# A row sum streamed through one core: one row per partition loaded ahead of the blocks, fifteen left for the end

## The chip, the core and the metric

The kernel runs on one core of one Trainium2 chip. The metric is the device time of one execution in microseconds (us); lower is better. Three engines matter: VectorE (DVE in the profile), ScalarE (ACT) and SyncE (SP), which issues all transfers on one queue. The transfers themselves are carried out by the core's 16 DMA engines.

## The reference

```python
batch, seq, dim = 32, 512, 1024
x = np.random.randn(batch, seq, dim).astype(np.float32)
multiplier = 0.5

def reference(x, multiplier):
    return (np.sum(x, axis=-1) * multiplier).astype(np.float32)
```

So 16,384 rows of 1,024 floats (4 KB a row, 64 MB in all) are each summed and scaled, and 64 KB of results go back.

## The kernel before

**Tiling.** With 128 partitions, each partition has 128 rows (`rows`), cut into eight blocks of `B = 16` rows. The first `own = 112` rows of each partition are consecutive rows of x, so that partition p begins at row 112 p (`x_rows`); seven blocks come from there. A block is one load of 128 pieces of 64 KB (8 MB), and consecutive partitions read 448 KB apart. The remaining 2,048 rows of x are the eighth block (`x_last`): 16 consecutive rows per partition, 64 KB apart. Results go back the same way: `out_rows` for the first 112 columns of `res`, `out_last` for the last 16.

**Buffers.** Three buffers `xb0` to `xb2` of 64 KB per partition take turns. Block b's load waits until VectorE has reduced block b - 3. `sums` holds raw sums, `res` the scaled results, 128 columns each. A small tile `end` holds the last columns of the last row.

**Loads.** The helper `load` (L73 to L82) makes one transfer on SyncE's queue, with up to two waits: `free` (VectorE has read the buffer's former contents) and `behind` (an earlier load has landed). All loads show line L76. When the program is finished, `start_loads_at_entry` moves SyncE's leading loads, those that wait for nothing, into the program's entry block, ahead of the barrier that the engines pass there. In the kernel before, these are the loads of blocks 0, 1 and 2.

**The seven blocks.** For blocks 0 to 5, VectorE reduces the whole block in one instruction (L121) and scales the 16 sums into `res` (L127). Of block 6 VectorE takes eight rows in this way, and ScalarE the other eight with `act_row` (L85): one activation per row that multiplies by the constant and accumulates.

**The tail.** The eighth block comes in five loads, in this order: ten rows, four rows, then one row and 384 columns of the last row, then 352 and 288 columns of it into `end`. Their edges are `bounds` and `cuts`. Before them stands a wait of SyncE for block 4's reduction, whose buffer they use. The third also waits for block 5's reduction, the second for block 5's landing, the fourth for block 6's landing and the fifth for block 6's reduction. Then SyncE issues the early store, 112 columns of `res` (L169), which waits for the last scaled sums of VectorE and the last of ScalarE's eight rows. In the tail `on_act` lists the rows that go to ScalarE; the others go to VectorE with `dve_sum` (L95), which adds a row's halves and accumulates. The last row is summed in three parts; the third (`final`) folds the earlier two in. The last store, 16 columns of `res` (L195), waits for `final` and for ScalarE's last row, and SyncE ends by waiting for both stores.

Of the kernel before, what the change touches and what calls it, by code (L numbers as in the profile page):

```python
# [9 lines left out]
def kernel(  # L10
# [13 lines left out]
    nc = tc.nc  # L24
# [4 lines left out]
    P = nc.NUM_PARTITIONS  # L29
# [3 lines left out]
    x_flat = x.flatten_outer_dims()  # L33
    N, D = x_flat.shape
    rows = N // P
    out_flat = out.rearrange("b s -> (b s)")
    mul = float(multiplier)

    B = 16
    n_blocks = rows // B  # L40
    assert N == P * rows and rows == n_blocks * B
    own = rows - B
    x_rows = x_flat[0 : P * own, :].rearrange("(p c) d -> p c d", p=P)
    x_last = x_flat[P * own : N, :].rearrange("(p c) d -> p c d", p=P)
    out_rows = out_flat[0 : P * own].rearrange("(p c) -> p c", p=P)
    out_last = out_flat[P * own : N].rearrange("(p c) -> p c", p=P)

    def sbuf(name, *shape):
        return ctx.enter_context(nc.sbuf_tensor(name, list(shape), fp32)).ap()
# [2 lines left out]
    buf = [sbuf(f"xb{i}", P, B, D) for i in range(bufs)]  # L52
    sums = sbuf("sums", P, rows)
    res = sbuf("res", P, rows)
    cuts = [384, 736, D]
    at = 368
    end = sbuf("end", P, at + D - cuts[1])

    def sem(name):
        return nc.alloc_semaphore(name=name)  # L60
# [5 lines left out]
    def marks(i, engine):  # L66

        s = dve_done if engine == "dve" else act_done
        i.then_inc(s, 1)
        counts[engine] += 1  # L70
        return counts[engine]

    def load(name, dst, src, free=None, behind=None):  # L73

        landed = sem(name)
        i = nc.sync.dma_start(out=dst, in_=src)  # L76
        if free is not None:
            i.wait_op(dve_done, free, "sem-ge")
        if behind is not None:
            i.wait_op(behind, 16, "sem-ge")  # L80
        i.then_inc(landed, 16)
        return landed  # L82

    def act_row(t, r, col):
        return nc.scalar.activation(  # L85
            out=t[:, r, :],
            in_=t[:, r, :],
            func=mybir.ActivationFunctionType.Copy,
            scale=mul,
            accum_out=res[:, col : col + 1],  # L90
        )

    def dve_sum(row, dst, scale):
        mid = row.shape[-1] // 2
        return nc.vector.tensor_tensor_reduce(  # L95
            out=row[:, 0:mid],
            in0=row[:, 0:mid],
            in1=row[:, mid:],
            scale=scale,
            scalar=0.0,  # L100
            op0=ADD,
            op1=ADD,
            accum_out=dst,
        )

    freed = []
    blocks = []
    for b in range(n_blocks - 1):
        c0 = b * B
        t = buf[b % bufs]  # L110
# [11 lines left out]
                out=sums[:, c0 : c0 + h], in_=t[:, 0:h, :], axis=mybir.AxisListType.X  # L122
# [5 lines left out]
            out=res[:, c0 : c0 + h],  # L128
            in_=sums[:, c0 : c0 + h],
# [12 lines left out]
    t = buf[(n_blocks - 1) % bufs]  # L142
    nc.sync.wait_ge(dve_done, freed[n_blocks - 1 - bufs])
    flat = t.rearrange("p c d -> p (c d)")
    flat_last = x_last.rearrange("p c d -> p (c d)")
    bounds = [0, 10 * D, 14 * D, 15 * D + cuts[0]]

    landed = [
        load(f"landed_p{k}", flat[:, lo:hi], flat_last[:, lo:hi], free, behind)
# [7 lines left out]
        )  # L157
    ]
    landed_end = [
        load(f"landed_e{k}", end[:, to : to + hi - lo], x_last[:, B - 1, lo:hi], free, behind)  # L160
        for k, (to, lo, hi, free, behind) in enumerate(
            (
                (0, cuts[0], cuts[1], None, blocks[n_blocks - 2]),
# [7 lines left out]
    early_stored = sem("early_stored")  # L171
    early.then_inc(early_stored, 16)

    on_act = {1, 4, 7, 9, 13, 14}
    for k, (lo, hi) in enumerate(((0, 10), (10, 14), (14, 15))):
        on = [r for r in range(lo, hi) if r in on_act]
        nc.scalar.wait_ge(landed[k], 16)
        for r in on:
            i = act_row(t, r, c0 + r)
        late_act = marks(i, "act") if k == len(landed) - 1 else None  # L180
        on = [r for r in range(lo, hi) if r not in on_act]
        nc.vector.wait_ge(landed[k], 16)
        for r in on:
            dve_sum(t[:, r, :], res[:, c0 + r : c0 + r + 1], mul)
    dve_sum(t[:, B - 1, 0 : cuts[0]], end[:, at - 2 : at - 1], 1.0)
    nc.vector.wait_ge(landed_end[0], 16)
    second = dve_sum(end[:, 0 : cuts[1] - cuts[0]], end[:, at - 1 : at], 1.0)

    second.then_inc(landed_end[1], 1)
    final = dve_sum(end[:, at - 2 :], res[:, rows - 1 : rows], mul)  # L190
    final.wait_op(landed_end[1], 17, "sem-ge")
    done = marks(final, "dve")

    nc.sync.wait_ge(act_done, late_act)
    store = nc.sync.dma_start(out=out_last, in_=res[:, own:])  # L195
    store.wait_op(dve_done, done, "sem-ge")
    stored = sem("stored")
    store.then_inc(stored, 16)
    nc.sync.wait_ge(early_stored, 16)
    nc.sync.wait_ge(stored, 16)  # L200

    def start_loads_at_entry(nc_):
# [61 lines left out]
```

## Time and profile before

| What | us |
|---|---|
| Runs: median of 3 (lowest to highest) | 160.75 (160.7 to 160.75) |
| The profiled execution: span from its first to its last instruction | 159.3 |
| VectorE busy | 119.8 (75%) |
| ScalarE busy | 16.3 (10%) |
| DMA queue of SyncE: share of the 16 engines' span | 98.1% |
| HBM read 67.11 MB, written 0.07 MB: mean rate over the span | 422 GB/s |

The page's parts used here are the chain of work that ended last, followed back from the last instruction; the timeline, which lists instructions in order of time with the idle time before each and what ended it; the issues of transfers with their size and the time from issue to landing; and the trace's records of DMA packets (start, duration, bytes). One packet here is the piece that goes to one partition. The slices of the DMA's busy share on the page swing between 6 and 9 tenths because a packet of 64 KB is counted where it starts; they are not stalls.

### The profile page before, as it was taken

What the parts mean: (1) busy time and instruction counts of PE and PEld (TensorE: products, weight loads), DVE (VectorE), ACT (ScalarE), POOL (GpSimd) and SP (SyncE); (2) the same over time, 40 slices, a digit from 0 to 9 for tenths busy, and PEclk for the clock granted to TensorE, in tenths of its full rate; (3) what the DMA queues carried; (4) which work ended last, traced back from release to release, by engine and by line L of the source; (5) the groups of instructions that cost most, each with busy time, mean ns of one, the idle gap of its engine ahead of it and who ended that gap; (6) DMA issues with size and microseconds to landing.
All of it is one profiled execution on the core that took longest, in us unless ns stands there. A gap on an engine that the chain in (4) does not pass through costs nothing.

```text
span 159.3 us, 123 instructions
## 1 busy us (share of the span) xinstructions
DVE 119.8 (75%) x38; ACT 16.3 (10%) x29; POOL 0.2 (0%) x4
## 2 busy tenths in 40 slices
DVE  0000059998699968999599995999959999598376
ACT  3000000000000000000000000000000000397384
POOL 0000000000000000000000000000000000000000
DMA  7996996997998969969969969969989799798994
GB/s 263 526 526 263 526 526 263 526 477 313 526 428 362 526 280 510 526 263 526 526 263 526 526 263 526 494 296 526 444 345 526 345 444 526 329 473 350 424 396 151
DMA packets 2016, 67.18 MB, mean 422 GB/s; under 512 B 480, under 2 KB 736, under 8 KB 864
## 3 DMA queue, kind: packets, MB, share of 16 engines
q1 hardware_dynamic: 2016, 67.18, 98.1%
HBM read 67.11 MB, written 0.07 MB: 422 GB/s over the span
## 4 chain that ended last, share of the span: by engine, by line
DMA 74%; DVE 24%; another core or an unknown queue 1%; SPq 0%; issue 0%
DMA xb<-in_x_dram 74%; DVE sums L121 22%; DVE xb L95 1%; DVE end L95 0%; SPq L76 0%; DVE res L127 0%; DVE res L95 0%
## 5 line engine op out<-in xcount | busy, mean ns | idle before, releaser
L121 DVE TENSOR_REDUCE sums<-xb 128x16 f32<-128x16384 f32 (+1 forms) x7 | 112.0, 16001 | 33.3 <-DMA xb<-in_x_dram 33.3
L85 ACT ACTIVATE xb<-xb 128x1024 f32<-128x1024 f32 x14 | 14.6, 1044 | 139.1 <-DMA xb<-in_x_dram 139.1
L95 DVE CUSTOM_DVE_ANT_0 xb<-xb 128x512 f32<-128x512 f32 (+1 forms) x10 | 6.0, 655 | 4.4 <-DMA xb<-in_x_dram 4.4
L85 ACT ACTIVATION_READ_ACCUMULATOR xb<-xb 128x1 f32 x14 | 2.6, 187 | 0.0
L85 ACT ACT_TABLE_LOAD x1 | 1.3, 1283 | 2.4 <-PEq L26 2.4
L127 DVE TENSOR_SCALAR res<-sums 128x16 f32<-128x16 f32 (+1 forms) x7 | 1.2, 174 | 0.2
L95 DVE DVE_READ_ACCUMULATOR2_ANT res<- 128x1 f32 x10 | 0.8, 82 | 0.0
L95 DVE CUSTOM_DVE_ANT_0 end<-end 128x176 f32<-128x176 f32 (+1 forms) x2 | 0.7, 326 | 0.0
L95 DVE DVE_READ_ACCUMULATOR2_ANT end<- 128x1 f32 x2 | 0.2, 82 | 0.0
L245 POOL MEMSET const-bfloat16-1.0<- 128x1 bf16 x1 | 0.1, 101 | 0.0
L245 POOL MEMSET const-uint8-127<- 128x1 uint8 x1 | 0.1, 101 | 0.0
L245 POOL MEMSET const-float32-0.0<- 128x1 f32 x1 | 0.1, 98 | 0.2 <-issue 0.2
L245 POOL MEMSET const-float32-1.0<- 128x1 f32 x1 | 0.1, 98 | 0.0
## 6 DMA issues: line engine op xcount, KB each, us to landing
xb<-in_x_dram SPq DMA_DIRECT2D x1, 5120.0 KB, 33.6
xb<-in_x_dram SPq DMA_DIRECT2D x1, 2048.0 KB, 36.4
xb<-in_x_dram SPq DMA_DIRECT2D x1, 704.0 KB, 20.8
end<-in_x_dram SPq DMA_DIRECT2D x1, 176.0 KB, 19.2
end<-in_x_dram SPq DMA_DIRECT2D x1, 144.0 KB, 10.8
xb<-in_x_dram SPq DMA_DIRECT2D x7, 40.8
out_dram<-res SPq DMA_DIRECT2D x1, 56.0 KB, 10.6
out_dram<-res SPq DMA_DIRECT2D x1, 8.0 KB, 1.4
```

The source lines that it names most:

```text
L85: return nc.scalar.activation(out=t[:, r, :], in_=t[:, r, :], func=mybir.ActivationFunctionType.Copy, scale=mul, accum_out=res[:, col : co ...
L95: return nc.vector.tensor_tensor_reduce(out=row[:, 0:mid], in0=row[:, 0:mid], in1=row[:, mid:], scale=scale, scalar=0.0, op0=ADD, op1=ADD, ...
L121: nc.vector.reduce_sum(out=sums[:, c0 : c0 + h], in_=t[:, 0:h, :], axis=mybir.AxisListType.X),
L127: scaled = nc.vector.tensor_single_scalar(out=res[:, c0 : c0 + h], in_=sums[:, c0 : c0 + h], scalar=mul, op=mybir.AluOpType.mult,)
L245: nc = _bacc.Bacc("TRN2", target_bir_lowering=False, num_devices=1)
```

## The change

One row per partition is taken out of the tail and put in front. The first 128 rows of x, consecutive, go one to each partition into a new tile `head` (512 KB in 128 pieces of 4 KB). This load stands first on SyncE's queue and waits for nothing, so it is moved to the entry block together with those of blocks 0, 1 and 2. ScalarE sums it before all else, into the last column of `res`. The seven blocks follow as before, starting 128 rows later. The tail has 15 rows per partition, 60 KB apart: nine rows, four, one and 384 columns, 352 columns, 288 columns. ScalarE gets one row less in the tail's first piece; VectorE gets as many as before. A second early store sends the 128 results of `head`, 4 bytes from each partition, to the first 512 bytes of the output. The last store has 15 columns instead of 16, and SyncE waits for three stores at the end.

```diff
     own = rows - B
-    x_rows = x_flat[0 : P * own, :].rearrange("(p c) d -> p c d", p=P)
-    x_last = x_flat[P * own : N, :].rearrange("(p c) d -> p c d", p=P)
-    out_rows = out_flat[0 : P * own].rearrange("(p c) -> p c", p=P)
-    out_last = out_flat[P * own : N].rearrange("(p c) -> p c", p=P)
+    tail = B - 1
+    x_head = x_flat[0:P, :]
+    x_rows = x_flat[P : P + P * own, :].rearrange("(p c) d -> p c d", p=P)
+    x_last = x_flat[P + P * own : N, :].rearrange("(p c) d -> p c d", p=P)
+    out_head = out_flat[0:P].rearrange("(p c) -> p c", p=P)
+    out_rows = out_flat[P : P + P * own].rearrange("(p c) -> p c", p=P)
+    out_last = out_flat[P + P * own : N].rearrange("(p c) -> p c", p=P)
...
+    head = sbuf("head", P, 1, D)
...
+    landed_head = load("landed_head", head[:, 0, :], x_head)
+    nc.scalar.wait_ge(landed_head, 16)
+    marks(act_row(head, 0, rows - 1), "act")
+
...
-    bounds = [0, 10 * D, 14 * D, 15 * D + cuts[0]]
+    bounds = [0, 9 * D, 13 * D, 14 * D + cuts[0]]
...
-        load(f"landed_e{k}", end[:, to : to + hi - lo], x_last[:, B - 1, lo:hi], free, behind)
+        load(f"landed_e{k}", end[:, to : to + hi - lo], x_last[:, tail - 1, lo:hi], free, behind)
...
+    early_head = nc.sync.dma_start(out=out_head, in_=res[:, rows - 1 :])
+    head_stored = sem("head_stored")
+    early_head.then_inc(head_stored, 16)
+
-    on_act = {1, 4, 7, 9, 13, 14}
-    for k, (lo, hi) in enumerate(((0, 10), (10, 14), (14, 15))):
+    on_act = {1, 4, 7, 12, 13}
+    for k, (lo, hi) in enumerate(((0, 9), (9, 13), (13, 14))):
...
-    dve_sum(t[:, B - 1, 0 : cuts[0]], end[:, at - 2 : at - 1], 1.0)
+    dve_sum(t[:, tail - 1, 0 : cuts[0]], end[:, at - 2 : at - 1], 1.0)
...
-    final = dve_sum(end[:, at - 2 :], res[:, rows - 1 : rows], mul)
+    final = dve_sum(end[:, at - 2 :], res[:, rows - 2 : rows - 1], mul)
...
-    store = nc.sync.dma_start(out=out_last, in_=res[:, own:])
+    store = nc.sync.dma_start(out=out_last, in_=res[:, own : rows - 1])
...
     nc.sync.wait_ge(early_stored, 16)
+    nc.sync.wait_ge(head_stored, 16)
     nc.sync.wait_ge(stored, 16)
```

## The prediction

> **What bounds the kernel now.** I read the chain of waits first, then the timeline, the SyncE queue's own timeline, the DMA issues, and last the trace's packet records. From the page (the chain, its first two lines):
>
> ```profile
> DMA 74%; DVE 24%; another core or an unknown queue 1%; SPq 0%; issue 0%
> DMA xb<-in_x_dram 74%; DVE sums L121 22%; DVE xb L95 1%; DVE end L95 0%; SPq L76 0%; DVE res L127 0%; DVE res L95 0%
> ```
>
> Taken at its word, this gives VectorE (DVE) a quarter of the span. The timeline (start, duration, engine, line, operation, and in brackets the idle time before it and who ended it) corrects that:
>
> ```profile
> 21.81 17.22 DVE L121 TENSOR_REDUCE sums<-xb 128x16 f32<-128x16384 f32 x1 [21.81 <-DMA xb<-in_x_dram]
> ...
> 41.15 17.22 DVE L121 TENSOR_REDUCE sums<-xb 128x16 f32<-128x16384 f32 x1 [1.91 <-DMA xb<-in_x_dram]
> ...
> 118.56 17.22 DVE L121 TENSOR_REDUCE sums<-xb 128x16 f32<-128x16384 f32 x1 [1.92 <-DMA xb<-in_x_dram]
> ...
> 137.91 8.69 DVE L121 TENSOR_REDUCE sums<-xb 128x8 f32<-128x8192 f32 x1 [1.92 <-DMA xb<-in_x_dram]
> ...
> 150.03 0.69 DVE L95 CUSTOM_DVE_ANT_0 xb<-xb 128x512 f32<-128x512 f32 x1 [3.23 <-DMA xb<-in_x_dram]
> ...
> 154.93 0.69 DVE L95 CUSTOM_DVE_ANT_0 xb<-xb 128x512 f32<-128x512 f32 x1 [1.13 <-DMA xb<-in_x_dram]
> ...
> 156.67 1.06 ACT L85 ACTIVATE xb<-xb 128x1024 f32<-128x1024 f32 x1 [0.59 <-DMA xb<-in_x_dram]
> ...
> 157.50 0.31 DVE L95 CUSTOM_DVE_ANT_0 end<-end 128x145 f32<-128x145 f32 x1
> ...
> 157.89 0.34 SPq L195 DMA_DIRECT2D out_dram<-res  x1
> ```
>
> Every block starts on VectorE after about 1.9 us of idleness that a landing ends. Landings are 19.35 us apart (137.91 - 21.81 = 116.10 over six blocks): 1.209 us for each row per partition (4 KB per partition, 512 KB over all). So one uninterrupted stream of loads sets the time, with four terms: the first landing, 2.46 us later than one block of stream (21.81 - 19.35); the stream; 0.41 us from the last landing (about 157.48) to the store's issue at 157.89; and 1.46 us to the end of the span at 159.35.
>
> The SyncE queue, at its start and towards the end:
>
> ```profile
> 0.00 1.34 SPq L76 DMA_DIRECT2D xb<-in_x_dram  x3
> ```
>
> ```profile
> 137.90 9.05 SPq L76 DMA_DIRECT2D end<-in_x_dram  x2
> 147.06 0.37 SPq L169 DMA_DIRECT2D out_dram<-res  x1
> 157.89 0.34 SPq L195 DMA_DIRECT2D out_dram<-res  x1
> ```
>
> The issues run far ahead of the data, except the last store. The DMA issues (KB each, us from issue to landing) show that a queued transfer's wait is not its cost:
>
> ```profile
> out_dram<-res SPq DMA_DIRECT2D x1, 56.0 KB, 10.6
> out_dram<-res SPq DMA_DIRECT2D x1, 8.0 KB, 1.4
> ```
>
> The 56 KB store took 10.6 us because five loads stood before it; the 8 KB one met an empty queue.
>
> **The change, part by part.** The bytes read are the same, so only where they lie and how they are cut can matter.
>
> *One row moves from the tail's first piece to a load of its own.* Removed: one of ten rows, 1.209 us. Added: a one-row load in 4 KB packets. Its extra comes from the tail. Ten rows took 12.12 us (150.03 - 137.91) against 12.09 by rate, 0.03 over; four rows 4.90 against 4.84, 0.06 over; 1.375 rows 1.74 against 1.66, 0.08 over. The packet records say why: each of the 16 engines takes 8 packets per load, and mean packet times are 2418 ns for 64 KB (steady), 613 for 16 KB, 218 for 5632 B, 60 for 1408 B, 51 for 1152 B. That is about 27.2 bytes per ns plus 8 to 10 ns a packet. Eight more packets per engine make about 0.07 us, and the end of a load a few ns (the packet before a block's boundary is 7 ns longer). I take **+0.08 us**, on the path, since the stream has no slack; bounds from these rows 0.03 and 0.10.
>
> *Its place at the front.* In the first wave of 64 KB packets the starts lie between 1.03 and 1.96 us and the mean is 3.10 us against 2.42 afterwards: a fill of 0.68 us. The wave's ends are spread over 0.36 us (4.16 to 4.53), and this spread is still there at the last load (semaphore steps from 157.10 to 157.47): the last engine sets the end. The trace has no cold start with 4 KB packets. If the fill is a wait for the first bytes it is paid once, whatever the packet: 0. If it belonged to the large packet, at best all 0.68 us would go. If it were paid again between the one-row load and the first block, +0.68 us. The second issue begins 0.43 us after the first, so by the first one's spread its packets can start at 1.46 to 2.39 us, while the eight small ones (about 1.27 us) occupy an engine until 1.03 + 0.68 + 1.27 = 2.98 us or longer. The next descriptors are there in time; I take 0 and keep -0.68 and +0.68.
>
> The Trainium skill speaks against so small a load: "DMA: Bandwidth & Descriptors", section "Anatomy of one DMA — SWDGE (gpsimd) path", gives a DMA a fixed 2.0 us beside its bytes (fitted there to another issuing path); by it, my estimate would be +2.0 us. The tail's queued loads, 0.03 to 0.08 us over rate, show this cost hidden; only the first landing, 2.46 us late, agrees with it.
>
> *SyncE issues one more load at entry*, 0.43 us with 0.05 us of gap (three took 1.34). The other engines pass the entry barrier some 0.48 us later: ScalarE's (ACT's) table load goes from 2.40 to 2.88. VectorE first has work at 21.81, a cover of 19 us. Everything behind in SyncE's queue waits on VectorE or on landings, so only the shift of the stream reaches it.
>
> *ScalarE's row moves to the start.* The new load should land near 2.46 + 1.28 = 3.74 us, the table load ends near 4.16, and one row costs 1.04 + 0.19 = 1.23 us: done by 5.5. ScalarE is then idle until about 139, and the result is read near 148. Nothing; 1.23 us if that cover were gone. At the other end ScalarE has three rows instead of four in the tail's first piece, before a landing it waited 0.63 us for: nothing.
>
> *Waits further on.* Blocks land 1.28 us later and the buffers come free 1.28 us later; the load into a freed buffer was issued at 39.06 with its predecessors in the queue until 60.5, a margin of 21 us that stays. The last load, issued at 146.6, moves to 147.9 and is needed at about 156.5. The early store moves from 147.06 to 148.3. By the time the nine-row piece lands, the shift is back to 0.08 us.
>
> *The second early store*, 128 pieces of 4 bytes. SyncE spends about 0.4 us on it where it otherwise waited 10.4 us. Its packets stand behind the 448-byte ones (25 ns each, the last ended at 157.17) and ahead of the last store's (158.73 to 158.93): 1.56 us of cover. At the 10.5 ns of a 64-byte packet they need 8 x 10.5 = 0.08 us; they reach the path above 195 ns apiece. Its semaphore wait stands before the one that ends last. I take 0.
>
> *The last store has 15 columns*: pieces of 60 bytes at a pitch of 60 instead of 64 at 64, so pieces share 64-byte lines. Not in the trace. Low bound 0 (4 bytes less is under 1 ns); if a packet becomes two, 8 x 10.5 = 0.08 us; if each line had to be read first, one fill, 0.68 us. I take 0.02, being nearest to the 64-byte row.
>
> *The tail's row pitch* goes from 64 KB to 60 KB. The 16 KB packets at the old pitch ran at 27.2 bytes per ns less the 8 ns, as fast as the blocks at 448 KB: no slow pitch to mend, 0. The same page of the Trainium skill, section "Latency and other measured facts", has copies fall to half the rate at large power-of-two pitches (it lists 512 KB and more). Were 64 KB such a pitch, leaving it would gain time; the rows say it is not.
>
> **Sum.** 0.08 + 0.02 = +0.10 us: span 159.35 to 159.45. The median of the runs, 160.75, is 1.40 us over the span, which I carry unchanged: **160.85 us**.
>
> **Rivals.**
> 1. *The stream restarts behind the one-row load* (slower). The small packets drain before the first block's descriptors or bytes arrive. Decides if those start later than about 2.98 us. Price 0.68: 160.75 + 0.08 + 0.68 = 161.5. For: the late starts reach 1.96 us, so three engines have little margin. Against: in the tail, loads of 51 ns packets follow without a gap. The Trainium skill's fixed cost, in full, would make it 162.8 by my estimate.
> 2. *The last store pays for its 60-byte pieces* (slower). It is alone on the path, so each ns counts. Price up to 0.68: about 161.5, half that 161.2. For: its 1.46 us are already mostly latency. Against: 64-byte packets at 10.5 ns show no read.
> 3. *The start gets shorter* (faster). Small first packets bring the engines into step, or the fill shrinks. Spread gone: 160.85 - 0.36 = 160.5; fill gone: 160.85 - 0.68 = 160.2. Against: two of the three latest starters (1.39, 1.66) end the wave last, which looks like late descriptors, and the number of these (128) is unchanged.
> 4. *The tiny store holds up the last one* (slower): above 195 ns a packet; at 250 ns, 8 x 55 = 0.44 us, 161.3.
>
> **Chances.** Forecast 0.45, rival 1 0.17, rival 2 0.15, rival 3 0.20, rival 4 0.03. A measurement here tells about 0.2%, 0.32 us, from no change: 160.43 to 161.07. The forecast (own range 160.7 to 161.05) lies within. Of rival 3 I give 0.16 to a gain beyond the bound; of rivals 1, 2 and 4 (0.35), 0.29 beyond it. Another 0.02 on each side comes out of the forecast for what I overlook. Faster 0.18, same 0.51, slower 0.31. The range, 160.35 to 161.5, leaves about a tenth at each end.
>
> **What would show it.** Right: a first block landing near 23.1 us (1.28 later), blocks 19.35 us apart, the nine-row piece landing at about 150.1, the last store again 1.46 us from issue to end. Rival 1: first block beyond 23.5. Rival 3: below 22.8, or a narrower spread of semaphore steps. Rivals 2 and 4: the last store's landing over 1.6 us, with its first packets late in rival 4 alone. The forecast is wrong if the end moves by more than 0.32 us.

## The result and the profile after

| | Before | After |
|---|---|---|
| Median of the runs, us | 160.74 (160.66 to 160.84) | 164.70 (163.99 to 166.16) |
| Ratio | | 1.0259, interval 1.0238 to 1.0280 |
| Profiled execution: span, us | 159.35 | 163.01 |
| Last store: issue, and from there to the end of the span, us | 157.89, 1.46 | 157.68, 5.33 |

The change makes the kernel 2.6% slower, outside the predicted range. The last row has all of it: the loads and the arithmetic ended 0.21 us earlier, and the end after the last store's issue grew by 3.87 us: -0.21 + 3.87 = 3.66 = 163.01 - 159.35.

The timeline of the changed kernel, in the same columns as before:

```profile
22.80 17.22 DVE L129 TENSOR_REDUCE sums<-xb 128x16 f32<-128x16384 f32 x1 [22.80 <-DMA xb<-in_x_dram]
...
138.92 8.69 DVE L129 TENSOR_REDUCE sums<-xb 128x8 f32<-128x8192 f32 x1 [1.92 <-DMA xb<-in_x_dram]
...
149.83 0.69 DVE L99 CUSTOM_DVE_ANT_0 xb<-xb 128x512 f32<-128x512 f32 x1 [2.02 <-DMA xb<-in_x_dram]
...
154.72 0.69 DVE L99 CUSTOM_DVE_ANT_0 xb<-xb 128x512 f32<-128x512 f32 x1 [1.14 <-DMA xb<-in_x_dram]
...
157.32 0.31 DVE L99 CUSTOM_DVE_ANT_0 end<-end 128x145 f32<-128x145 f32 x1
...
157.68 0.33 SPq L207 DMA_DIRECT2D out_dram<-res  x1
```

The blocks are still 19.35 us apart (138.92 - 22.80 = 116.12 over six). The whole stream lies about 0.2 us earlier than the change's bytes alone would put it, already at the first block.

The page's DMA issues after the change (the three stores), and the two rows of SyncE's waits that concern the end:

```profile
out_dram<-res SPq DMA_DIRECT2D x1, 56.0 KB, 14.4
out_dram<-res SPq DMA_DIRECT2D x1, 0.5 KB, 14.3
out_dram<-res SPq DMA_DIRECT2D x1, 7.5 KB, 5.3
```

```profile
SPq L206 <- ACT xb L89: 8.7, 1, 8.7
SPq L212 <- DMA out_dram<-res: 4.8, 1, 4.8
```

Before, the same wait for the stores (SyncE's waits of the kernel before) was:

```profile
SPq L200 <- DMA out_dram<-res: 1.1, 1, 1.1
```

The last store takes 5.3 us from issue to landing where it took 1.4, and the early store of 56 KB 14.4 where it took 10.6, although its own size is as before and the loads ahead of it end no later. The small one between them is new. The semaphore steps in the trace (each engine reports its share of a store; the expectations call these reports receipts) show the place more finely. The four-byte store's sixteen reports come from 157.37 to 162.79 us, four of the early store's only from 160.59 to 162.50, and the last store's from 158.98 to 162.96; before, the last store's came within 0.17 us. The packet records of the four-byte store, in contrast, are 9 ns each and all over by 157.04, and the last store's packets begin 0.83 us after its issue (158.51), as before (0.84). The chain of waits of this execution ends at 157.63 with VectorE; it doesn't show this wait.

### The profile page after: what moved, and what is told of

It is laid out like the page before. It is cut to its first block, busy times and chain, and to the rows that moved or that the text cites. A ratio compares the mean times of both kernels' runs of the same rounds, so it can differ in the third digit from the quotient of the medians.

```text
span 163.0 us, 126 instructions
## 1 busy us (share of the span) xinstructions
DVE 119.9 (74%) x38; ACT 16.4 (10%) x29; POOL 0.2 (0%) x4
## 4 chain that ended last, share of the span: by engine, by line
DMA 72%; DVE 23%; another core or an unknown queue 1%; SPq 0%; issue 0%
DMA xb<-in_x_dram 72%; DVE sums L129 21%; DVE xb L99 1%; SPq L80 0%; DVE end L99 0%; DVE res L135 0%; DVE res L99 0%
## 5 line engine op out<-in xcount | busy, mean ns | idle before, releaser
L89 ACT ACTIVATE xb<-xb 128x1024 f32<-128x1024 f32 x13 | 13.6, 1046 | 138.4 <-DMA xb<-in_x_dram 138.4
L89 ACT ACTIVATE head<-head 128x1024 f32<-128x1024 f32 x1 | 1.1, 1056 | 0.0
## 6 DMA issues: line engine op xcount, KB each, us to landing
out_dram<-res SPq DMA_DIRECT2D x1, 56.0 KB, 14.4
```

Of the source, the lines that this page charges most:

```text
L89: return nc.scalar.activation(out=t[:, r, :], in_=t[:, r, :], func=mybir.ActivationFunctionType.Copy, scale=mul, accum_out=res[:, col : co ...
```

## The experiments

Four runs first separate the suspects: the four-byte store, and the last store's 60-byte pieces. Times are medians; the ratios and their intervals are worked out from the single runs, so that they can differ from the ratio of two medians in the last digits.

**Without the four-byte store.**

```diff
-    early_head = nc.sync.dma_start(out=out_head, in_=res[:, rows - 1 :])
-    head_stored = sem("head_stored")
-    early_head.then_inc(head_stored, 16)
...
-    nc.sync.wait_ge(head_stored, 16)
```

> The changed kernel without the store of the 128 four-byte results (the first 128 outputs are left unwritten). Theory T, the tiny store: 128 four-byte writes into one stretch of 512 bytes are done one after another, some 42 ns each (its semaphore steps after the change run from 157.37 to 162.79 us), and the last store's receipts wait behind them. Then the last store should end about 1.46 us after its issue, as before the change, and the whole should take 160.75 - 0.2 = 160.55 us, since the loads ended 0.19 us earlier. Rival L, the last store's 60-byte pieces: the time stays near 164.5 us, and the last store's semaphore steps stay spread over some 4 us.

160.63 us against 160.73, ratio 0.9999 (0.9989 to 1.0008). SyncE's wait and the DMA issues of the two stores left:

```profile
SPq L208 <- DMA out_dram<-res: 1.2, 1, 1.2
```

```profile
out_dram<-res SPq DMA_DIRECT2D x1, 56.0 KB, 9.4
out_dram<-res SPq DMA_DIRECT2D x1, 7.5 KB, 1.5
```

The last store with its 60-byte pieces is back to 1.5 us, and the early store ahead of it takes 9.4. Theory T holds, L falls.

**The kernel before with 60-byte pieces at the end.**

```diff
-    out_last = out_flat[P * own : N].rearrange("(p c) -> p c", p=P)
+    out_last = out_flat[P * own : P * own + P * (B - 1)].rearrange("(p c) -> p c", p=P)
...
-    store = nc.sync.dma_start(out=out_last, in_=res[:, own:])
+    store = nc.sync.dma_start(out=out_last, in_=res[:, own : rows - 1])
```

> The kernel before with its last store cut to 15 columns, 60-byte pieces at a pitch of 60 bytes (the last 128 outputs are left unwritten). Theory T: 160.75 us, at most 160.85. Rival L: 163 us or more, with the last store's semaphore steps spread over microseconds. In between: up to 0.7 us more, if every piece waits once for a line to be read.

160.71 us against 160.73, ratio 0.9999 (0.9990 to 1.0009). The last store's line of the DMA issues:

```profile
out_dram<-res SPq DMA_DIRECT2D x1, 7.5 KB, 1.4
```

The 60-byte pieces cost nothing that can be measured.

**The kernel before with a four-byte store added.**

```diff
     early.then_inc(early_stored, 16)
+    scratch = nc.dram_tensor("scratch", [P, 1], fp32, kind="Internal").ap()
+    extra = nc.sync.dma_start(out=scratch, in_=res[:, 0:1])
+    extra_stored = sem("extra_stored")
+    extra.then_inc(extra_stored, 16)
...
     nc.sync.wait_ge(early_stored, 16)
+    nc.sync.wait_ge(extra_stored, 16)
     nc.sync.wait_ge(stored, 16)
```

> The kernel before with one store added behind the early one: 128 four-byte pieces of one column of results into 512 consecutive bytes of a scratch tensor in HBM. Theory T: 163.5 to 166 us, 3 to 5 us over before, with the last store's receipts as late as after the change, though its pieces are 64 bytes. Rival L: 160.75 us.

164.63 us against 160.73, ratio 1.0250 (1.0235 to 1.0266): nearly the whole loss, with nothing else of the change. SyncE's waits and the DMA issues:

```profile
SPq L204 <- DMA scratch<-res: 5.3, 1, 5.3
```

```profile
out_dram<-res SPq DMA_DIRECT2D x1, 56.0 KB, 16.3
scratch<-res SPq DMA_DIRECT2D x1, 0.5 KB, 16.1
out_dram<-res SPq DMA_DIRECT2D x1, 8.0 KB, 5.9
```

The last store's 64-byte pieces suffer in the same way as the 60-byte ones.

**The four-byte store in the middle of the stream.** It is taken from its place and issued before block 3's load.

```diff
         t = buf[b % bufs]
+        if b == bufs:
+            early_head = nc.sync.dma_start(out=out_head, in_=res[:, rows - 1 :])
+            early_head.wait_op(act_done, 1, "sem-ge")
+            head_stored = sem("head_stored")
+            early_head.then_inc(head_stored, 16)
...
-    early_head = nc.sync.dma_start(out=out_head, in_=res[:, rows - 1 :])
-    head_stored = sem("head_stored")
-    early_head.then_inc(head_stored, 16)
```

> The changed kernel with the four-byte store issued just ahead of the load of block 3, so that its packets stand in the queue between blocks 2 and 3, at about 61 us. Theory T with posted writes: the 5.4 us pass beside the loads, and the whole takes 160.55 us. Theory T with writes that stop the DMA engine they are on: block 3 lands up to 5 us later and the whole takes 161 to 166 us. Rival L: near 164.5 us.

166.32 us against 160.73, ratio 1.0344 (1.0315 to 1.0372): worse than at the end. The store's issue and the timeline around block 3:

```profile
5.33 0.35 SPq L120 DMA_DIRECT2D out_dram<-res  x1
...
61.66 17.22 DVE L134 TENSOR_REDUCE sums<-xb 128x16 f32<-128x16384 f32 x1 [1.97 <-DMA xb<-in_x_dram]
...
85.92 17.22 DVE L134 TENSOR_REDUCE sums<-xb 128x16 f32<-128x16384 f32 x1 [6.83 <-DMA xb<-in_x_dram]
...
105.28 17.22 DVE L134 TENSOR_REDUCE sums<-xb 128x16 f32<-128x16384 f32 x1 [1.93 <-DMA xb<-in_x_dram]
```

Blocks 2 and 3 are 24.26 us apart instead of 19.35: the store holds up the loads queued behind it for 4.9 us, on all sixteen engines (block 3's semaphore steps lie within 0.65 us). Its own reports come from 61.49 to 67.19. The packet records show where the time goes: block 3's first packets begin on time (60.81 to 61.31), but the first two of each engine, 4.84 us together otherwise, take 9.5 to 10.1. On some engines the first takes 2.4 us and the second 7.3, on others 7.1 and 2.6, so an engine whose first packet was not slowed lost the time in its second. That is the second of the expectations in its direction, somewhat above its 161 to 166 us, but no engine got away with less. Loads do not cover this store in the one place that was tried.

**What it is about the pieces that costs.** Six runs of the kernel before with the added store in other shapes. Only the scratch tensor and the slices differ. For 4-byte pieces 512 bytes apart:

```diff
-    scratch = nc.dram_tensor("scratch", [P, 1], fp32, kind="Internal").ap()
-    extra = nc.sync.dma_start(out=scratch, in_=res[:, 0:1])
+    scratch = nc.dram_tensor("scratch", [P, 128], fp32, kind="Internal").ap()
+    extra = nc.sync.dma_start(out=scratch[:, 0:1], in_=res[:, 0:1], allow_slow_non_contiguous=True)
```

For 64 bytes apart the tensor has 16 columns instead of 128. For half as many pieces:

```diff
-    extra = nc.sync.dma_start(out=scratch, in_=res[:, 0:1])
+    extra = nc.sync.dma_start(out=scratch[0:64, :], in_=res[0:64, 0:1])
```

For 8, 16 and 32 bytes the tensor and the slice of `res` have two, four and eight columns, all stored.

> The kernel before with the added store of 128 four-byte pieces, this time 512 bytes apart in the scratch tensor. Theory S, neighbours: the pieces wait for one another because they share lines of HBM, so apart they run side by side: 160.75 to 161.3 us, receipts within about 0.5 us. Rival N, number: every write under some size costs some 43 ns in a single place, wherever it lies: about 164.6 us, as with the dense ones (164.63).

> The kernel before with an added store of 128 pieces of 32 bytes, consecutive in scratch (4 KB in all). Theory S: what counts is how many pieces share a line; with 64-byte lines two pieces share one, and the 60-byte store with such sharing cost nothing (160.71 against 160.73), so 160.75 to 161.2 us. If the shared stretch is 512 bytes, 16 pieces share one but eight stretches go side by side: an eighth of the dense cost, 0.5 us or less, hidden behind the 1.2 us that the last store needs: 160.75 us. Rival N, the number of small writes: 164.6 us.

> The kernel before with 64 four-byte pieces (partitions 0 to 63) into 256 consecutive bytes of scratch. Reading 1, one place does all pieces in turn at 43 ns: 64 x 43 = 2.75 us, receipts from about 157.2 to 160.0, and 161.2 to 162 us in all. Reading 2, each line of 64 bytes does its 16 pieces in turn at 5.5 / 16 = 0.34 us each, and lines go side by side: as long as with 128 pieces, 5.5 us, and about 164.6 us.

> The kernel before with 128 four-byte pieces 64 bytes apart in scratch, one to a line of 64 bytes, eight to a stretch of 512. If only the line of 64 bytes is shared (reading 2): the added store's receipts are complete within 0.6 us, as with 512 bytes apart, and 160.75 us. If pieces of one 512-byte stretch wait for each other and stretches go side by side: 8 x 43 ns = 0.35 us more, still 160.75 to 160.9 us. If all pieces of a store under 8 KB go in turn: 164.6 us.

> The kernel before with 128 pieces of 8 bytes, consecutive in scratch (1 KB). Reading 2: eight pieces to a line of 64 bytes, 8 x 0.34 = 2.75 us of receipts, 161.2 to 162 us. Reading 1 (number of pieces in one place): 5.5 us and 164.6 us; if the place is a stretch of 512 bytes, 2.75 us as well.

> The kernel before with 128 pieces of 16 bytes, consecutive in scratch (2 KB), four to a line of 64 bytes. If every piece of a 64-byte line costs 0.34 us in turn, as with 8 bytes (eight to a line, receipts over some 2.4 us) and 4 bytes (sixteen, over 5 to 6 us): the added store's receipts are complete 1.4 us after its first, at about 158.8 us instead of 157.8, and the whole takes 160.75 to 160.9 us, since the last store's packets only start at 158.7. If the shared unit is 32 bytes, or only pieces of different DMA engines disturb each other: receipts complete by 158.0 us, and 160.75 us.

| Added store | Pieces in 64 bytes | Its semaphore steps, us | Time and that of before, us | Ratio |
|---|---|---|---|---|
| 128 x 4 bytes, consecutive | 16 | 157.46 to 163.52 | 164.63, 160.73 | 1.0235 to 1.0266 |
| 64 x 4 bytes, consecutive | 16 | 157.39 to 161.62 | 164.24, 160.80 | 1.0200 to 1.0246 |
| 128 x 8 bytes, consecutive | 8 | 157.46 to 159.87 | 161.60, 160.80 | 1.0033 to 1.0068 |
| 128 x 16 bytes, consecutive | 4 | 157.42 to 158.24 | 160.74, 160.76 | 0.9988 to 1.0008 |
| 128 x 32 bytes, consecutive | 2 | 157.32 to 157.95 | 160.83, 160.79 | 0.9995 to 1.0014 |
| 128 x 4 bytes, 64 apart | 1 | 157.38 to 157.78 | 160.71, 160.80 | 0.9984 to 1.0002 |
| 128 x 4 bytes, 512 apart | 1 | 157.38 to 157.90 | 160.77, 160.79 | 0.9991 to 1.0010 |

(The profiled execution of the half store took 163.24 us, the shortest of its four.) The size of a piece and their number are not it: 128 pieces of four bytes cost nothing once they lie 64 bytes apart, and half as many next to each other cost almost as much as all. Neighbourhood is: theory S, and the first reading by number falls. The law is not quite what the second reading has. Eight pieces in 64 bytes took 2.4 us where it says 2.75, but four spread the reports over 0.81 us, some 0.3 more than the 0.4 to 0.5 of the stores apart, where it says 1.4 in all. (Part of each spread is that of the engines themselves: the last load's steps are spread over 0.38 to 0.61 us in these seven runs.) Whether the shared unit is 64 or 32 bytes, and whether it matters that pieces from several DMA engines meet in one unit, stays open, and so does what in the chip takes the time.

The DMA issues of the 8-byte store beside those of the store 64 bytes apart show the same on the page:

```profile
scratch<-res SPq DMA_DIRECT2D x1, 1.0 KB, 12.4
out_dram<-res SPq DMA_DIRECT2D x1, 8.0 KB, 2.2
```

```profile
scratch<-res SPq DMA_DIRECT2D x1, 0.5 KB, 10.4
out_dram<-res SPq DMA_DIRECT2D x1, 8.0 KB, 1.4
```

**The small gain at the start.** The kernel before, with block 0 cut into one row and fifteen; the first row's pieces stay 448 KB apart.

```diff
+        cut = 1 if b == 0 else 0
+        if cut:
+            first = load("landed_first", t[:, 0:cut, :], x_rows[:, c0 : c0 + cut, :])
+            nc.vector.wait_ge(first, 16)
         landed = load(
             f"landed{b}",
-            t,
-            x_rows[:, c0 : c0 + B, :],
+            t[:, cut:, :],
+            x_rows[:, c0 + cut : c0 + B, :],
```

> The kernel before with block 0 loaded in two pieces, one row per partition (4 KB packets, 448 KB apart) and then 15, nothing else changed. The changed kernel's loads ended 0.19 to 0.24 us earlier although its stream should be 0.07 us longer. Theory F: small first packets shorten the fill, wherever they lie: first block's landing 21.5 to 21.65 instead of 21.8, and 160.4 to 160.6 us. Rival C, consecutive rows: with the rows 448 KB apart nothing is gained: first landing 21.85, 160.8 us.

160.58 us against 160.79, ratio 0.9990 (0.9981 to 0.9998). The first block on VectorE:

```profile
21.68 17.22 DVE L125 TENSOR_REDUCE sums<-xb 128x16 f32<-128x16384 f32 x1 [21.68 <-DMA xb<-in_x_dram]
```

The last semaphore step of block 0 is at 21.59 us; in the nine profiles with an uncut block 0 in front it is between 21.67 and 21.99. In the four profiles with the consecutive row in front (the changed kernel and its variants), less the row's 1.21 us, it is 21.55 to 21.65. So a small first load shortens the start by about 0.2 us in both placings of its rows; theory F holds. The effect is small: the quickest start of an uncut block, 21.67, is only 0.08 us later. Why it does so was not tried, nor whether the size of the first load counts or only that there are two.

**The change without tiny pieces.** VectorE turns the column of 128 results into four rows of 32 while it waits for block 0, and the store has four pieces of 128 bytes.

```diff
+    column = sbuf("column", P, 32)
+    lines = sbuf("lines", P, 32)
...
-    marks(act_row(head, 0, rows - 1), "act")
+    cleared = sem("cleared")
+    nc.vector.memset(column[:, :], 0.0).then_inc(cleared, 1)
+    nc.scalar.wait_ge(cleared, 1)
+    summed = marks(act_row(head, 0, 0, column[:, 0:1]), "act")
+    turned = sem("turned")
+    nc.vector.wait_ge(act_done, summed)
+    nc.vector.transpose(lines[:, :], column[:, :]).then_inc(turned, 1)
...
-    early_head = nc.sync.dma_start(out=out_head, in_=res[:, rows - 1 :])
+    early_head = nc.sync.dma_start(
+        out=out_flat[0:P].rearrange("(a c) -> a c", c=32), in_=lines[0:P:32, :]
+    )
+    early_head.wait_op(turned, 1, "sem-ge")
```

> The changed kernel with the 128 first results turned on VectorE (a 32x32 transpose of one column into four rows, at about 6 us, where it is idle) and stored as four pieces of 128 bytes instead of 128 of 4. Theory T (only the tiny pieces cost): as without that store, 160.5 to 160.65 us. Rival: any further store between the early and the last one costs receipts in order, then 161 us or more.

160.56 us against 160.79, ratio 0.9985 (0.9976 to 0.9993): some 0.2 us less than the kernel before, and over 4 us less than the changed one. The rival falls: four pieces of 128 bytes between the early and the last store cost nothing that can be measured. The timeline near the start and SyncE's wait at the end:

```profile
5.59 0.21 DVE L120 STREAM_TRANSPOSE lines<-column 128x32 f32<-128x32 f32 x1 [2.56 <-ACT head L91]
```

```profile
SPq L224 <- DMA out_dram<-res: 1.0, 1, 1.0
```

The turn costs 0.21 us in 17 us of idle time, and the wait for the stores is 1.0 us.

## Why the prediction was wrong

**The step that failed is the second early store**, "I take 0". It priced 128 pieces of 4 bytes at a 64-byte packet's 10.5 ns, 0.08 us behind a cover of 1.56 us, and counted the store as done with its packets. The packet's duration was even smaller (9 ns), but it is not the write's cost: the reports came over 5.4 us, and those of the last store with them. Without this store the time was 160.63 us, and with such a store added to the kernel before 164.63. From the last packet's record to the last report it was 5.75 us (157.04 to 162.79); by an engine's eight packets that is some 0.7 us apiece, over three times the 195 ns from which the step itself said that they reach the path. "DMA: Bandwidth & Descriptors" of the Trainium skill, section "Anatomy of one DMA — SWDGE (gpsimd) path", says of another issuing path that a semaphore is not updated until the last byte is confirmed at its target; the gap between 157.04 and 162.79 agrees. Rival 4 had the place, but not the mechanism: it had the store's packets keep the last store's waiting, and its own sign, late first packets of the last store, did not come (0.83 us after the issue, 0.84 before). The sign that it shared with rival 2, a landing over 1.6 us, came with 5.3 us. Its chance of 0.03 and its price of 0.44 us went by packet durations as well. The row nearest in size, 64-byte pieces, had one piece to 64 bytes and so couldn't show what sixteen do: the same 128 pieces 64 bytes apart cost nothing (160.71 us).

**The last store's 15 columns**: right, about nothing, and rival 2 falls; 0.02 was no more than noise.

**The one-row load**: its packets took 159 ns where they did not wait, as the tail's rows had it (8 to 10 ns over their bytes). The nine rows took 149.83 - 138.92 = 10.91 us, 0.03 over rate, as ten rows had; so the 0 for the tail's row pitch was right too.

**The place at the front**: 0 was chosen, and the size was off: the first block began at 22.80 instead of near 23.1. That fits rival 3's shorter fill, at about 0.3 us of the 0.68 it could have been at most: the first wave of 64 KB packets took 2.57 us on average instead of 3.10, with 2.42 afterwards. The spread between the engines did not shrink (0.47 us at block 0's landing, against 0.36). With 0.07 us more of stream, 0.19 to 0.21 us stayed. Rival 1, a restart of the stream, did not come: the block's packets began between 2.41 and 2.78 us, before 2.98. The one-row load, with nothing queued ahead of it, landed 3.2 us after its issue, but the block behind it was not held up by it. The fixed 2.0 us of the Trainium skill (the same page and section) and 1.2 us for its 512 KB make 3.2 us as an estimate, so the landing agrees.

**Entry, ScalarE's row, the waits further on**: as worked out. The table load began at 2.86 us (2.88 forecast), the early store was issued at 148.07 (148.3, less the shorter start), and none of it reached the end.

So the sum of the other terms, corrected by the fill, is 160.85 - 0.3 = 160.55 us. The kernel without the four-byte store measured 160.63 and the one with the turned store 160.56. Even without the failed step, then, the forecast would have been 0.2 to 0.3 us too high.

## What to carry to other kernels

A store's packet durations don't price it: read the semaphore steps, and expect microseconds where many tiny pieces from different partitions land side by side in one short stretch of HBM (here over 5 us for 128 pieces of 4 bytes). Results that are one number to a partition should leave the chip turned into rows, or beside other columns, in pieces of tens of bytes (here 16 or more, four or fewer to 64 bytes, cost nothing measurable). Loads queued behind such a store did not hide it here, and it also delayed the reports of the stores ahead of and behind it.

## What was not expected of the hardware

- The reports of 128 four-byte pieces in 512 consecutive bytes were spread over 5.4 to 6.1 us; those of the same pieces 64 bytes apart over 0.4 us.
- With that store between two loads, all sixteen engines lost about 4.9 us, also the one that had reported its share of it first, at 61.49 us.
- Reports of an earlier store on the same queue were held as well: four of the early store's came after 160.5 us, though its packets ended by 156.98.
- A first load in 4 KB packets shortened the start of the stream by about 0.2 us (block 0 landed at 21.59 us instead of 21.67 to 21.99), consecutive or 448 KB apart.
